# Rows of 64 KB in three buffers, loads on SyncE's queue and stores on ScalarE's in a written-out order

## The chip, the cores and the metric

The kernel runs on one core of a Trainium2 chip. The metric is device time in microseconds (us). A transfer "lands" when all its data has arrived and an engine that waits for it may start. In the profile lines DVE is VectorE, ACT ScalarE, POOL GpSimd, SP SyncE, PE TensorE and PEld its weight loads; L77 is line 77 of the kernel, and a q after an engine's name is its queue of DMA issues. "Span" is the length of the one profiled execution; in the profiled runs of the kernels tried here the reported time is 1.7 to 2.2 us longer than the span. Ratios are those over the fast runs of both kernels in the same rounds, so they are not quite the ratio of the medians that are quoted.

## The reference

```python
x: 16 x 3 x 512 x 512 float32; factor = 1.5
mean = np.mean(x, axis=(2, 3), keepdims=True)
return np.clip(mean + factor * (x - mean), 0, 1)
```

There are 48 images of 1 MiB (262,144 pixels). Each must be read whole before its first pixel can be written, because the mean is needed. The traffic is 50.33 MB in and 50.33 MB out, whatever the kernel does.

## The kernel before

Eleven tiles of four images and two of two images; a row (one partition) is 32 KB in the large tiles. VectorE sums the rows, one small matmul adds the rows of an image and gives all of them the mean times (1 - factor), ScalarE computes relu(factor * x + bias), VectorE clips at 1. Loads go out on SyncE's queue, stores on GpSimd's. A scheduler orders each engine's instructions.

```python
TILE_IMGS = [4] * 11 + [2, 2]
X_BUFS = 5
STORE_ENGINE = "gpsimd"
# ... [blockw: a 128 x 128 block-diagonal matrix of (1 - factor) / n_pix]
xpool = ctx.enter_context(tc.tile_pool(name="xpool", bufs=X_BUFS))
# ... [small pools]
for i, N in enumerate(TILE_IMGS):
    FREE = n_pix * N // P
    # ... [src, dst: FREE contiguous elements per partition]
    nc.sync.dma_start(out=xt, in_=src)
    nc.vector.tensor_reduce(out=rsum, in_=xt, axis=..., op=add)
    nc.tensor.matmul(pbias, blockw[N], rsum, start=True, stop=True)
    nc.scalar.copy(out=bias, in_=pbias)
    nc.scalar.activation(out=xt, in_=xt, func=Relu, bias=bias, scale=factor)
    nc.vector.tensor_scalar(out=xt, in0=xt, scalar1=1.0, scalar2=None, op0=min)
    store_eng.dma_start(out=dst, in_=xt)
```

## Time and profile before

| | before |
|---|---|
| time, median | 240.24 us (240.1 to 240.93, 3 runs) |
| span of the profiled run | 238.6 us |
| bytes moved, mean rate | 100.66 MB, 422 GB/s |
| busy: VectorE, ScalarE | 66%, 37% |
| a load and a store of 4.19 MB, steady state | 19.4 us |

The page of the kernel before: the busy times, then the span in 40 slices (DMA is the mean busy share of the 16 DMA engines in tenths, GB/s what they moved), then the packets.

```profile
span 238.6 us, 238 instructions
...
PE 7.4 (3%) x26; PEld 6.5 (3%) x26; DVE 156.5 (66%) x26; ACT 89.1 (37%) x27; POOL 10.3 (4%) x25
...
DMA  7999999999999999999999999999999999999995
GB/s 269 434 439 439 439 439 352 439 434 439 439 439 439 439 434 434 423 428 412 423 439 439 434 439 439 439 439 439 434 428 426 426 404 428 431 434 439 428 434 214
DMA packets 3744, 100.66 MB, mean 422 GB/s; under 512 B 416, under 2 KB 416, under 8 KB 416
```

The DMA row stands at 9 from the second slice to the last but one, and the rate is 434 to 439 GB/s where nothing disturbs it. No compute engine comes near that. The Trainium skill ("DMA: Bandwidth & Descriptors", Where 436 GB/s comes from) gives 435 GB/s as the ceiling of the ports through which DMA reaches SBUF, the on-chip memory; the trace shows 439, about 1% more. So the kernel before is bound by its bytes: 100.66 MB at 439 GB/s are 229.3 us, and start, end and dips take the other 9.

The groups of instructions of the kernel before: busy us and mean ns of one after the first bar, idle time of the engine before them after the second.

```profile
L77 DVE TENSOR_REDUCE rsum<-xt 128x1 f32<-128x8192 f32 x11 | 95.5, 8685 | 56.1 <-DMA xt<-in_x_dram 56.1
L90 ACT ACTIVATE xt<-xt,bias 128x8192 f32<-128x8192 f32 x11 | 78.4, 7124 | 0.4
L97 DVE TENSOR_SCALAR xt<-xt 128x8192 f32<-128x8192 f32 x11 | 48.6, 4417 | 0.0
...
L85 PE MATMUL pbias<-rsum,blockw 128*128 128x1 f32 x26 | 7.4, 355 | 209.5 <-DVE rsum L77 209.5
```

A 4 MB tile takes 8.7 us of reduce, 7.1 of relu and 4.4 of clip. These 20 us overlap with other tiles' transfers, so they cost nothing as long as DMA always has something queued. Stretches of the end of the kernel before: length, then busy us and number of instructions for PE, PEld, DVE, ACT, POOL, then clock, DMA share and GB/s.

```profile
195.00:206.00 11.00, 0.56 (x2) 0.50 (x2) 9.39 (x3) 7.35 (x3) 1.22 (x2) 1.00 0.99 420
206.00:216.00 10.00, 0.00 (x0) 0.00 (x0) 5.86 (x2) 0.00 (x0) 2.31 (x2) 1.00 0.97 419
216.00:226.00 10.00, 0.56 (x2) 0.50 (x2) 2.52 (x2) 3.87 (x2) 0.53 (x1) 1.00 1.03 442
226.00:236.00 10.00, 0.00 (x0) 0.00 (x0) 0.00 (x0) 0.00 (x0) 0.00 (x0) 1.00 0.94 403
```

The last load (2 MB) lands at 211.8 us and the last store is issued at 223.5, but DMA has older stores to move all the while: 419 to 442 GB/s.

### The profile page before, as it was taken

What the parts mean: (1) busy time and instruction counts of PE and PEld (TensorE: products, weight loads), DVE (VectorE), ACT (ScalarE), POOL (GpSimd) and SP (SyncE); (2) the same over time, 40 slices, a digit from 0 to 9 for tenths busy, and PEclk for the clock granted to TensorE, in tenths of its full rate; (3) what the DMA queues carried; (4) which work ended last, traced back from release to release, by engine and by line L of the source; (5) the groups of instructions that cost most, each with busy time, mean ns of one, the idle gap of its engine ahead of it and who ended that gap; (6) DMA issues with size and microseconds to landing.
All of it is one profiled execution on the core that took longest, in us unless ns stands there. A gap on an engine that the chain in (4) does not pass through costs nothing.

```text
span 238.6 us, 238 instructions
## 1 busy us (share of the span) xinstructions
PE 7.4 (3%) x26; PEld 6.5 (3%) x26; DVE 156.5 (66%) x26; ACT 89.1 (37%) x27; POOL 10.3 (4%) x25
## 2 busy tenths in 40 slices
PE   0000000000000000000000000000000000000000
PEld 0000000000000000000000000000000000000000
DVE  0088999999599079459629909917945979742300
ACT  2002966472906601900920650470190095406000
POOL 2000001000000000000000000000000000500000
DMA  7999999999999999999999999999999999999995
GB/s 269 434 439 439 439 439 352 439 434 439 439 439 439 439 434 434 423 428 412 423 439 439 434 439 439 439 439 439 434 428 426 426 404 428 431 434 439 428 434 214
DMA packets 3744, 100.66 MB, mean 422 GB/s; under 512 B 416, under 2 KB 416, under 8 KB 416
## 3 DMA queue, kind: packets, MB, share of 16 engines
q1 hardware_dynamic: 1872, 50.33, 49.4%
q0 software_dynamic: 1872, 50.33, 49.0%
HBM read 50.33 MB, written 50.33 MB: 422 GB/s over the span
## 4 chain that ended last, share of the span: by engine, by line
issue 38%; DMA 35%; DVE 18%; POOL 2%; POOLq 0%; SPq 0%
DMA xt<-in_x_dram 19%; DMA out_dram<-xt 16%; DVE rsum L77 11%; DVE xt L97 7%; POOL out_dram L104 2%; POOLq L137 0%; SPq L74 0%; POOLq L104 0%
## 5 line engine op out<-in xcount | busy, mean ns | idle before, releaser
L77 DVE TENSOR_REDUCE rsum<-xt 128x1 f32<-128x8192 f32 (+1 forms) x13 | 104.4, 8029 | 61.7 <-DMA xt<-in_x_dram 61.7
L90 ACT ACTIVATE xt<-xt,bias 128x8192 f32<-128x8192 f32 (+1 forms) x13 | 85.8, 6598 | 0.4
L97 DVE TENSOR_SCALAR xt<-xt 128x8192 f32<-128x8192 f32 (+1 forms) x13 | 53.2, 4091 | 5.0 <-ACT xt L90 5.0
L88 ACT COPY bias<-pbias 128x1 f32<-128x1 f32 x13 | 2.1, 160 | 130.6 <-PE pbias L85 130.6
L104 POOL DMA_DIRECT2D out_dram<-xt x13 | 9.0, 692 | 213.0 <-DVE xt L97 212.8
L85 PE MATMUL pbias<-rsum,blockw 128*128 128x1 f32 x26 | 7.4, 355 | 209.5 <-DVE rsum L77 209.5
L85 PEld LDWEIGHTS pbias<-rsum,blockw 128*128 128x128 f32 x26 | 6.5, 311 | 210.3 <-DVE rsum L77 107.1
L88 ACT ACT_TABLE_LOAD x1 | 1.3, 1283 | 0.8 <-PEq L123 0.8
L51 POOL MEMSET blockw<- 32x32 f32 (+1 forms) x6 | 0.8, 128 | 0.2
L49 POOL MEMSET blockw<- 128x128 f32 x2 | 0.3, 205 | 0.3 <-POOLq L123 0.3
L123 POOL MEMSET const-float32-0.0<- 128x1 f32 x1 | 0.1, 104 | 0.2 <-issue 0.2
L123 POOL MEMSET const-bfloat16-1.0<- 128x1 bf16 x1 | 0.1, 113 | 0.0
L123 POOL MEMSET const-uint8-127<- 128x1 uint8 x1 | 0.1, 113 | 0.0
L123 POOL MEMSET const-float32-1.0<- 128x1 f32 x1 | 0.1, 110 | 0.0
## 6 DMA issues: line engine op xcount, KB each, us to landing
xt<-in_x_dram SPq DMA_DIRECT2D x11, 4096.0 KB, 24.6
out_dram<-xt POOLq DMA_DIRECT2D x11, 4096.0 KB, 36.0
xt<-in_x_dram SPq DMA_DIRECT2D x2, 2048.0 KB, 19.5
out_dram<-xt POOLq DMA_DIRECT2D x2, 2048.0 KB, 19.1
```

Of the source, the lines that this page charges most:

```text
L49: nc.gpsimd.memset(wt, 0.0)
L51: nc.gpsimd.memset(wt[b * PPI : (b + 1) * PPI, b * PPI : (b + 1) * PPI], wconst)
L77: nc.vector.tensor_reduce(out=rsum, in_=xt, axis=mybir.AxisListType.X, op=mybir.AluOpType.add,)
L85: nc.tensor.matmul(pbias, blockw[N], rsum, start=True, stop=True)
L88: nc.scalar.copy(out=bias, in_=pbias)
L90: nc.scalar.activation(out=xt, in_=xt, func=mybir.ActivationFunctionType.Relu, bias=bias, scale=factor,)
L97: nc.vector.tensor_scalar(out=xt, in0=xt, scalar1=1.0, scalar2=None, op0=mybir.AluOpType.min,)
L104: store_eng.dma_start(out=dst, in_=xt)
L123: nc = _bacc.Bacc("TRN2", target_bir_lowering=False, num_devices=1)
```

## The change

It is meant to make the transfers as large as three buffers allow, to take the stores off GpSimd's software queue, and to fix the order of each engine's instructions by hand instead of leaving it to the scheduler. The sum is split: half of a row on VectorE, half on ScalarE. Relu and clip go in four chunks, so that they overlap within a tile.

```diff
-TILE_IMGS = [4] * 11 + [2, 2]
-X_BUFS = 5
-STORE_ENGINE = "gpsimd"
+ROW = 16384
+BUFS = 3
+HALF = ROW // 2
+CHUNK = 4096
+JUNK = 2048
 ... [block matrix written in another way; pools of 2]
+    def load(t):
+        xt = xpool.tile([P, ROW], f32, name="xt")
+        nc.sync.dma_start(out=xt, in_=dram(x_f, t))
+    def compute(t):
+        nc.vector.tensor_reduce(out=sums[:, 0:1], in_=xt[:, 0:HALF], ...)
+        for j in range(n_act):
+            nc.scalar.activation(out=junk, in_=xt[:, a : a + JUNK], func=Act.Copy,
+                                 accum_out=sums[:, 1 + j : 2 + j])
+        for j in range(1 + n_act):
+            nc.tensor.matmul(pbias, blockw, sums[:, j : j + 1], start=j == 0, stop=j == n_act)
+        nc.scalar.copy(out=bias, in_=pbias)
+        for c in range(0, ROW, CHUNK):
+            nc.scalar.activation(out=part, in_=part, func=Act.Relu, bias=bias, scale=factor)
+            nc.vector.tensor_scalar(out=part, in0=part, scalar1=1.0, scalar2=None, op0=Alu.min)
+    def store(t):
+        nc.scalar.dma_start(out=dram(out_f, t), in_=tiles.pop(t))
+    with tc.manual_schedule():
+        for t in range(min(BUFS, n_tiles)):
+            load(t)
+        for t in range(n_tiles):
+            compute(t)
+            store(t)
+            if t + BUFS < n_tiles:
+                load(t + BUFS)
```

With 16,384 elements per partition a tile is eight images, 8.39 MB, and there are six tiles.

More of the change, by code (lines that the diff above doesn't have):

```diff
@@ L5 @@
 import concourse.tile as tile
-from concourse import bass_utils, mybir
+from concourse import mybir
 from concourse._compat import with_exitstack
-TILE_IMGS = [4] * 11 + [2, 2]
-X_BUFS = 5
-STORE_ENGINE = "gpsimd"
+P = 128
+ROW = 16384
[3 more added lines that the diff above has]
+JUNK = 2048
 @with_exitstack
@@ L23 @@
     nc = tc.nc
-    P = 128
+    f32 = mybir.dt.float32
+    Alu = mybir.AluOpType
+    Act = mybir.ActivationFunctionType
     B, C, H, W = x.shape
-    n_img = B * C
-    n_pix = H * W
+    n_img, n_pix = B * C, H * W
+    ppi = n_pix // ROW
+    per_tile = P // ppi
+    n_tiles = n_img // per_tile
+    assert ppi * ROW == n_pix and per_tile * n_tiles == n_img
     factor = float(factor)
-    f32 = mybir.dt.float32
-    assert sum(TILE_IMGS) == n_img
-    NMAX = max(TILE_IMGS)
+    wconst = (1.0 - factor) / float(n_pix)
@@ L36, with dram @@
     x_f = x.rearrange("b c h w -> (b c h w)")
     out_f = out.rearrange("b c h w -> (b c h w)")
-    wconst = (1.0 - factor) / float(n_pix)
+    def dram(ap, t):
+        return bass.AP(tensor=ap.tensor, offset=t * P * ROW, ap=[[ROW, P], [1, ROW]])
     consts = ctx.enter_context(tc.tile_pool(name="consts", bufs=1))
-    blockw = {}
-    for N in sorted(set(TILE_IMGS)):
-        wt = consts.tile([P, P], f32, name=f"blockw{N}")
-        PPI = P // N
-        if N == 1:
-            nc.gpsimd.memset(wt, wconst)
-        else:
-            nc.gpsimd.memset(wt, 0.0)
-            for b in range(N):
-                nc.gpsimd.memset(wt[b * PPI : (b + 1) * PPI, b * PPI : (b + 1) * PPI], wconst)
-        blockw[N] = wt
@@ L54 @@
-    xpool = ctx.enter_context(tc.tile_pool(name="xpool", bufs=X_BUFS))
-    rpool = ctx.enter_context(tc.tile_pool(name="rpool", bufs=12))
-    bpool = ctx.enter_context(tc.tile_pool(name="bpool", bufs=12))
-    psum = ctx.enter_context(tc.tile_pool(name="psum", bufs=8, space=bass.MemoryType.PSUM))
-    if STORE_ENGINE == "sync":
-        store_eng = nc.sync
-    elif STORE_ENGINE == "act":
-        store_eng = nc.scalar
-    else:
-        store_eng = nc.gpsimd
-    pix_off = 0
-    for i, N in enumerate(TILE_IMGS):
-        FREE = n_pix * N // P
-        npix_tile = n_pix * N
-        xt = xpool.tile([P, NMAX * n_pix // P], f32, name="xt")[:, :FREE]
-        src = bass.AP(tensor=x_f.tensor, offset=pix_off, ap=[[FREE, P], [1, FREE]])
-        dst = bass.AP(tensor=out_f.tensor, offset=pix_off, ap=[[FREE, P], [1, FREE]])
-        nc.sync.dma_start(out=xt, in_=src)
-        rsum = rpool.tile([P, 1], f32)
+    xpool = ctx.enter_context(tc.tile_pool(name="xpool", bufs=BUFS))
@@ new lines @@
+    jpool = ctx.enter_context(tc.tile_pool(name="jpool", bufs=1))
+    rpool = ctx.enter_context(tc.tile_pool(name="rpool", bufs=2))
+    bpool = ctx.enter_context(tc.tile_pool(name="bpool", bufs=2))
+    psum = ctx.enter_context(tc.tile_pool(name="psum", bufs=2, space=bass.MemoryType.PSUM))
+    blockw = consts.tile([P, P], f32, name="blockw")
+    nc.gpsimd.memset(blockw, 0.0)
+    for a in range(0, P, 2 * ppi):
+        mid, end = a + ppi, a + 2 * ppi
+        nc.gpsimd.memset(blockw[a:end, mid:end], wconst)
+        nc.gpsimd.memset(blockw[a:mid, mid:end], 0.0)
+        nc.gpsimd.memset(blockw[a:mid, a:mid], wconst)
@@ L77 @@
+    tiles = {}
+    def load(t):
+        xt = xpool.tile([P, ROW], f32, name="xt")
+        nc.sync.dma_start(out=xt, in_=dram(x_f, t))
+        tiles[t] = xt
+    def compute(t):
+        xt = tiles[t]
+        n_act = (ROW - HALF) // JUNK
+        sums = rpool.tile([P, 1 + n_act], f32, name="sums")
         nc.vector.tensor_reduce(
-            out=rsum,
-            in_=xt,
-            axis=mybir.AxisListType.X,
-            op=mybir.AluOpType.add,
-        )
-        pbias = psum.tile([P, 1], f32)
@@ L85 @@
-        nc.tensor.matmul(pbias, blockw[N], rsum, start=True, stop=True)
-        bias = bpool.tile([P, 1], f32)
-        nc.scalar.copy(out=bias, in_=pbias)
-        nc.scalar.activation(
-            out=xt,
-            in_=xt,
-            func=mybir.ActivationFunctionType.Relu,
-            bias=bias,
-            scale=factor,
-        )
-        nc.vector.tensor_scalar(
-            out=xt,
-            in0=xt,
-            scalar1=1.0,
-            scalar2=None,
-            op0=mybir.AluOpType.min,
-        )
@@ L104 @@
-        store_eng.dma_start(out=dst, in_=xt)
-        pix_off += npix_tile
+            out=sums[:, 0:1], in_=xt[:, 0:HALF], axis=mybir.AxisListType.X, op=Alu.add
+        )
+        for j in range(n_act):
+            junk = jpool.tile([P, JUNK], f32, name="junk")
+            a = HALF + j * JUNK
+            nc.scalar.activation(
+                out=junk, in_=xt[:, a : a + JUNK], func=Act.Copy, accum_out=sums[:, 1 + j : 2 + j]
+            )
+        pbias = psum.tile([P, 1], f32, name="pbias")
@@ new lines, in compute @@
+        for j in range(1 + n_act):
+            nc.tensor.matmul(pbias, blockw, sums[:, j : j + 1], start=j == 0, stop=j == n_act)
+        bias = bpool.tile([P, 1], f32, name="bias")
+        nc.scalar.copy(out=bias, in_=pbias)
+        for c in range(0, ROW, CHUNK):
+            part = xt[:, c : c + CHUNK]
+            nc.scalar.activation(out=part, in_=part, func=Act.Relu, bias=bias, scale=factor)
+            nc.vector.tensor_scalar(out=part, in0=part, scalar1=1.0, scalar2=None, op0=Alu.min)
```

## The prediction

> **What bounds it now.** The DMA engines. The page moves 100.66 MB at 422 GB/s; its slices show DMA at 0.9 or more nearly throughout, at 434 to 439 GB/s, with VectorE busy 66% and ScalarE 37%. The Trainium skill ("DMA: Bandwidth & Descriptors", Where 436 GB/s comes from) gives 435 GB/s for a core's 16 engines; the trace agrees (439). At 439 GB/s the bytes need 229.3 of the 238.6 us span. By the windows about 2.5 us go at the start, 2.5 at the end, the rest in dips (352 GB/s where the first store begins). So nothing can win more than 2 to 3%. No compute wait matters: in steady state a 4 MB load and store complete every 19.4 us, VectorE working 13.1 of it.
>
> **What the change does.**
> - Six tiles of 8.39 MB (19.1 us of DMA each way at 439 GB/s) instead of eleven of 4.19 and two of 2.10 MB. Bytes are unchanged.
> - Three buffers: a load waits for the landed store three tiles earlier.
> - Stores move from GpSimd's software queue to ScalarE's hardware queue. The same page (Issuing engines are not separate DMA queues) says that all queues share the same 16 engines: no bandwidth gained. The trace agrees: loads and stores, both backlogged, advance equally, 19.4 us per tile.
> - Half of the sum goes to ScalarE (4 x 2048), relu and clip in four chunks. Engines work tile by tile in written order: no reduce of the next tile before this tile's last clip.
>
> **Compute of one tile, landing to store issue.** Reduce of 8192: 8.69 us, ScalarE's sums about as long (estimate 4 x 2.1, from 7.12 us at 8192 and 3.71 at 4096). Five matmuls instead of one, and the bias copy: 1 to 2.5 us (one pair takes 0.56). Relu 4 x 3.65; last clip 2.29. Sum about 28 us, under the 38.2 us in which DMA moves one tile in and one out: mid-run DMA stays full.
>
> **Critical path.** Load 0 lands at 22.7 us (the second load's landing before). Store 0 issues at about 51, store 1 at about 80, just as store 0 ends: hardly a gap. Then load t+3 shares with store t+1 and queues stay filled until load 5 lands. By then six loads, four stores and a bit of the fifth have moved, 85 MB: at before's pace (83.3 MB by 195 us) 198 to 200 us. Store 4 then runs alone and ends near 215 to 218, while tile 5 computes until about 227: a DMA hole of about 10 us. Then store 5 alone, 19 to 21 us (the last stores of before ran at 400 to 450 GB/s), plus about 3 us of issue and landing. Span about 250; the reported time lies 1.6 above the span, as now.
>
> **Predicted: 251.5 us, 8 in 10 between 246.5 and 256.5. Faster by over 2%: 0.03; within 2%: 0.09; slower by over 2%: 0.88.**
>
> **What would show it.** Slices: DMA full until about 215, a hole of 8 to 12 us, a last full stretch of about 20; last load landing at 196 to 201; the chain of waits ending in last load, about 28 us of tile 5's compute, last store; relu chunks 3.6 to 3.7 us; ScalarE sums 2.0 to 2.3 us each; mid-run still about 435 to 440 GB/s.
>
> **What would make it wrong.** Loads taking more than half of the bandwidth: load 5 lands earlier, the hole shrinks, 240 to 245 us. A hardware store queue that lifts the dips: 3 to 4 us less. A DMA gap after store 0 because tile 1 computes longer, or ScalarE held up at its store's issue: a few us more.

## The result

| | before | after |
|---|---|---|
| time, median | 240.17 us (4 runs) | 254.78 us (253.09 to 258.41, 4 runs); the three fast ones 253.09 to 255.92, mean 254.22 |
| ratio | | 1.0581 (95%: 1.0524 to 1.0638) |
| span of the profiled run | 238.6 us | 251.3 us |
| mean rate | 422 GB/s | 401 GB/s |
| packets | 3744 | 1729 |
| busy: VectorE, ScalarE | 66%, 37% | 43%, 55% |

The change makes the kernel 5.8% slower. The same lines of the page, after:

```profile
span 251.3 us, 317 instructions
...
PE 13.7 (5%) x60; PEld 13.2 (5%) x60; DVE 107.0 (43%) x30; ACT 137.3 (55%) x79; POOL 1.4 (1%) x17
...
DMA  8979899799989899989999899997999979303994
GB/s 334 501 334 501 355 480 501 334 355 480 480 355 501 344 396 428 501 355 480 407 428 501 355 480 407 429 501 344 490 417 417 501 344 490 167 0 167 501 490 177
DMA packets 1729, 100.67 MB, mean 401 GB/s; under 512 B 192, under 2 KB 192, under 8 KB 192
```

Two things are to be seen. First, the rates swing between 334 and 501. That is partly the ruler: there are half as many packets, so each now carries a row of 64 KB and, at a sixteenth of 439 GB/s, keeps its engine for 2.4 us (an estimate), a good part of a 6.3 us slice. Bytes are counted in such lumps: 16 packets of 64 KB in a slice of 6.28 us are 167 GB/s, and 334 and 501 are two and three times that. Only longer stretches can be compared. Secondly, near the end there are slices with 167, 0 and 167 GB/s. The stretches of the end, after:

```profile
206.00:211.00 5.00, 0.90 (x5) 0.90 (x5) 4.05 (x1) 3.37 (x4) 0.00 (x0) 1.00 0.97 419
211.00:216.00 5.00, 1.40 (x7) 1.31 (x7) 0.00 (x0) 3.54 (x2) 0.00 (x0) 1.00 0.97 419
216.00:229.50 13.50, 0.00 (x0) 0.00 (x0) 9.18 (x4) 11.13 (x4) 0.00 (x0) 1.00 0.00 0
229.50:240.00 10.50, 0.00 (x0) 0.00 (x0) 0.00 (x0) 0.00 (x0) 0.00 (x0) 1.00 0.93 399
```

From 216 to 229.5 us not a byte moves, while ScalarE (11.1 us of 13.5) and VectorE (9.2) work on the last tile. These 13.5 us can be laid beside the whole difference of the two spans, 12.7 us. The chain of waits says what goes on in them (start, length, what):

```profile
157.73 43.54 DMA xt<-in_x_dram
...
201.36 8.70 DVE sums L77
...
210.10 2.31 PE pbias L88 x10
...
212.43 0.17 ACT bias L90
...
212.62 14.52 ACT xt L93 x4
...
227.16 2.29 DVE xt L94
```

The last load is issued at 157.7 us, since only then its buffer has been stored, and lands at 201.3. Then reduce, matmuls, bias copy, four relus and the last clip follow one another, 28.2 us, and only at 229.5 the store of the whole tile is issued; it lands 20.7 us later. The store of the tile before was all that DMA had in the meantime, and it was done at 216. The groups, after:

```profile
L93 ACT ACTIVATE xt<-xt,bias 128x4096 f32<-128x4096 f32 x24 | 87.0, 3697 | 0.2
L83 ACT ACTIVATE junk<-xt 128x2048 f32<-128x2048 f32 x24 | 45.8, 1910 | 71.8 <-DMA xt<-in_x_dram 65.8
L94 DVE TENSOR_SCALAR xt<-xt 128x4096 f32<-128x4096 f32 x24 | 55.1, 2294 | 61.5 <-ACT xt L93 61.5
L77 DVE TENSOR_REDUCE sums<-xt 128x1 f32<-128x8192 f32 x6 | 52.1, 8683 | 61.0 <-DMA xt<-in_x_dram 61.0
L88 PE MATMUL pbias<-sums,blockw 128*128 128x1 f32 x60 | 13.7, 354 | 198.7 <-DVE sums L77 198.7
...
L83 ACT ACTIVATION_READ_ACCUMULATOR junk<-xt 128x1 f32 x24 | 4.5, 186 | 0.0
```

Each part costs about what the trace before led to expect. The Trainium skill ("ScalarE: Activation LUTs", What ACT_TABLE_LOAD costs) gives 186 ns + 0.833 ns per element for an ACTIVATE with immediate scale and bias and about 280 ns + 0.833 ns per element with a bias per partition. An estimate worked out from that is 1892 ns for 2048 and 3692 ns for 4096 elements. The trace has 1910 and 3697.

### The profile page after: what moved, and what is told of

It is laid out like the page before. It is cut to its first block, busy times and chain, and to the rows that moved or that the text cites. A ratio compares the mean times of both kernels' runs of the same rounds, so it can differ in the third digit from the quotient of the medians.

```text
span 251.3 us, 317 instructions
## 1 busy us (share of the span) xinstructions
PE 13.7 (5%) x60; PEld 13.2 (5%) x60; DVE 107.0 (43%) x30; ACT 137.3 (55%) x79; POOL 1.4 (1%) x17
## 2 busy tenths in 40 slices
DMA packets 1729, 100.67 MB, mean 401 GB/s; under 512 B 192, under 2 KB 192, under 8 KB 192
## 4 chain that ended last, share of the span: by engine, by line
DMA 42%; ACT 18%; another core or an unknown queue 15%; DVE 13%; PE 3%; issue 0%; SPq 0%; DVEq 0%
DMA xt<-in_x_dram 26%; ACT xt L93 17%; DMA out_dram<-xt 16%; DVE sums L77 10%; PE pbias L88 3%; DVE xt L94 3%; ACT bias L90 0%; SPq L70 0%; DVEq L77 0%
## 5 line engine op out<-in xcount | busy, mean ns | idle before, releaser
L93 ACT ACTIVATE xt<-xt,bias 128x4096 f32<-128x4096 f32 x24 | 87.0, 3697 | 0.2
L83 ACT ACTIVATE junk<-xt 128x2048 f32<-128x2048 f32 x24 | 45.8, 1910 | 71.8 <-DMA xt<-in_x_dram 65.8
L94 DVE TENSOR_SCALAR xt<-xt 128x4096 f32<-128x4096 f32 x24 | 55.1, 2294 | 61.5 <-ACT xt L93 61.5
L77 DVE TENSOR_REDUCE sums<-xt 128x1 f32<-128x8192 f32 x6 | 52.1, 8683 | 61.0 <-DMA xt<-in_x_dram 61.0
L88 PE MATMUL pbias<-sums,blockw 128*128 128x1 f32 x60 | 13.7, 354 | 198.7 <-DVE sums L77 198.7
L88 PEld LDWEIGHTS pbias<-sums,blockw 128*128 128x128 f32 x60 | 13.2, 329 | 199.1 <-DVE sums L77 167.7
L90 ACT COPY bias<-pbias 128x1 f32<-128x1 f32 x6 | 1.0, 159 | 17.0 <-PE pbias L88 17.0
L83 ACT ACTIVATION_READ_ACCUMULATOR junk<-xt 128x1 f32 x24 | 4.5, 186 | 0.0
L63 POOL MEMSET blockw<- 16x16 f32 x4 | 0.4, 104 | 0.2
L64 POOL MEMSET blockw<- 16x16 f32 x4 | 0.4, 104 | 0.0
## 6 DMA issues: line engine op xcount, KB each, us to landing
xt<-in_x_dram SPq DMA_DIRECT2D x6, 43.5
```

The costliest lines, as they stand in the source:

```text
L63: nc.gpsimd.memset(blockw[a:mid, mid:end], 0.0)
L64: nc.gpsimd.memset(blockw[a:mid, a:mid], wconst)
L77: nc.vector.tensor_reduce(out=sums[:, 0:1], in_=xt[:, 0:HALF], axis=mybir.AxisListType.X, op=Alu.add)
L83: nc.scalar.activation(out=junk, in_=xt[:, a : a + JUNK], func=Act.Copy, accum_out=sums[:, 1 + j : 2 + j])
L88: nc.tensor.matmul(pbias, blockw, sums[:, j : j + 1], start=j == 0, stop=j == n_act)
L93: nc.scalar.activation(out=part, in_=part, func=Act.Relu, bias=bias, scale=factor)
```

## The experiments

The theory: DMA sets the time, and what the change adds is a stretch in which DMA has nothing to do, because the last tile is so large that its compute outlasts the stores that were still queued. Put as a sum, the hole is the time from the last landing to the last store's issue, less the time that DMA needs for the stores still waiting at that landing. The rivals: the 64 KB rows make DMA slower throughout; ScalarE's queue is worse than GpSimd's; the written-out order costs; the number of buffers alone is to blame.

### The last tile stored in four chunks

```diff
     def store(t):
-        nc.scalar.dma_start(out=dram(out_f, t), in_=tiles.pop(t))
+        xt = tiles.pop(t)
+        if t < n_tiles - 1:
+            nc.scalar.dma_start(out=dram(out_f, t), in_=xt)
+            return
+        for c in range(0, ROW, CHUNK):
+            dst = ...  # columns c to c + CHUNK of tile t
+            nc.sync.dma_start(out=dst, in_=xt[:, c : c + CHUNK])
```

> The changed kernel, but the last tile is stored in four column chunks from SyncE's queue, each as soon as its clip is done. Theory (the whole loss is the DMA hole from 216 to 229.5 us, in which tile 5 computes and nothing can be stored): the first chunk can go at about 219 us instead of 229.5, the hole shrinks to about 3 us, span about 240.5, time about 242 (0.95 of the changed kernel). Rival (the 64 KB rows or ScalarE's store queue make DMA slower throughout): the tail gives back less than 3 us, time 250 or more.

Measured: 243.37 us (243.1 to 243.74), ratio to before 1.0132 (1.0094 to 1.0169), span 242.0. The stretches:

```profile
216.00:219.00 3.00, 0.00 (x0) 0.00 (x0) 1.28 (x1) 3.00 (x2) 0.00 (x0) 1.00 0.25 109
219.00:222.00 3.00, 0.00 (x0) 0.00 (x0) 1.70 (x2) 3.00 (x2) 0.00 (x0) 1.00 0.41 175
222.00:230.00 8.00, 0.00 (x0) 0.00 (x0) 5.39 (x3) 6.49 (x2) 0.00 (x0) 1.00 1.01 426
```

The first chunk goes out at 220.0 us, and from 222 on DMA is full. From 216 to 222 us, 109 and 175 GB/s over 3 us each make 0.85 MB, what full DMA moves in 2 us: the hole is worth about 4 us instead of 13.5. The means of the fast runs fall by 10.8 us, from 254.22 to 243.39, and the hole by about 9.5; the 1.3% that is left goes with the hole that is left. So nearly the whole loss sat in the hole. Both chunking and the queue of this one store changed. The run with GpSimd's stores below shows no effect of the queue there; SyncE's was not tried by itself.

### Half the tile, twice the buffers

```diff
-ROW = 16384
-BUFS = 3
+ROW = 8192
+BUFS = 6
```

> The changed kernel with rows of 32 KB and six buffers: same buffer bytes, same queues, same written order, half the tile. Theory (granularity): compute of one tile falls from 28 to about 16 us and at the last load's landing several computed tiles are still to be stored, so no DMA hole: span 237 to 239, time 238.5 to 241, level with before. Rival (hardware store queue or written order costs): 248 or more, DMA slices below 435 GB/s in mid-run.

Measured: 240.19 us, ratio to before 0.9997 (0.9954 to 1.0041), 421 GB/s. The last load lands at 207.9 us and the last store is issued at 223.8, and from the middle of the run to the last slice but one the slices stay at 411 to 439 GB/s. Stores on ScalarE's queue, the split sum, the chunks (now two of a row) and the written order are all still there and cost nothing. What costs is the size of the tile, or how few of them fit.

### Half the tile, still three buffers; and four

```diff
-ROW = 16384
+ROW = 8192
```

> The changed kernel with rows of 32 KB, still three buffers. Theory: with three buffers, when the last load lands only one tile (9.6 us alone) is left to store while the last tile computes about 16 us: a hole of about 6 us, half of that of the changed kernel, plus a gap of 2 to 3 us after the first store: time 246 to 249. If it were the tile size alone and not how many tiles lie ready: 239 to 241. If it were the buffer count alone and not the size: 254.

Measured: 255.06 us (253.95 to 255.55), ratio 1.0609: as slow as the changed kernel. This misses the 246 to 249 that I had expected. The stretches show in which way:

```profile
41.00:47.00 6.00, 0.00 (x0) 0.00 (x0) 4.70 (x3) 3.25 (x3) 0.00 (x0) 1.00 0.59 202
124.50:183.60 59.10, 4.32 (x18) 4.07 (x18) 27.02 (x9) 34.39 (x21) 0.00 (x0) 1.00 0.98 413
...
234.00:241.00 7.00, 0.00 (x0) 0.00 (x0) 4.59 (x2) 4.58 (x2) 0.00 (x0) 1.00 0.00 0
```

The hole at the end is there and has the expected size: the last load lands at 225.0 us, the store before it is done at 234, the last one is issued at 240.9, so 7 us stand empty. But the middle loses as much again. At 41 to 47 us only 202 GB/s move, and from 124.5 to 183.6 the mean is 413 GB/s against 433 in the copies below. The chain of waits runs through store, load and compute of every third tile without a break; one round of it (start, length, what):

```profile
60.44 21.05 DMA out_dram<-xt
...
81.56 23.03 DMA xt<-in_x_dram
...
104.71 4.43 DVE sums L77
...
110.85 7.32 ACT xt L93 x2
...
118.19 2.31 DVE xt L94
...
120.52 22.05 DMA out_dram<-xt
```

Every third store is issued at 60.4, 120.5, 181.5 and 240.9 us, so one buffer's round takes about 59 to 61 us, while DMA needs 57.3 for three tiles both ways at 439 GB/s (an estimate from the rate of before). The reading is that the round, and not DMA, then sets the pace; it asks that one more buffer fill the middle, which the next run shows. (The changed kernel's round, from the store at 78.8 us to the one at 190.8, takes 112 us beside 114.7: it just fits, and 426 GB/s move in it, the rate of the 64 KB copy below from 60 to 220 us.) The middle of the run had been checked only by comparing the compute of one tile with its DMA. Here that comparison comes out well too (15.7 us under 19.1), so it is not enough: the round has to fit as well.

Four buffers were tried with

```diff
-ROW = 16384
-BUFS = 3
+ROW = 8192
+BUFS = 4
```

> Rows of 32 KB with four buffers, between the runs with three (255.1) and six (240.2). Theory: at the last landing two tiles (2 x 9.6 us of DMA) are still to be stored, more than the 15.8 us from landing to store issue, so no tail hole, and four buffers also cover load, compute and store in mid-run: 239.5 to 242.5. If the loss shrank evenly with the buffers: about 250.

Measured: 244.5 us (243.29 to 244.61), ratio 1.0173 (1.0142 to 1.0204), span 242.5. This misses the 239.5 to 242.5 that I had expected; whether it is slower by 2% is unclear. The middle is full now (433 to 434 GB/s from 100 to 215 us). The hole is smaller, not gone:

```profile
225.00:228.00 3.00, 0.00 (x0) 0.00 (x0) 1.91 (x1) 3.00 (x1) 0.00 (x0) 1.00 0.56 240
228.00:230.00 2.00, 0.00 (x0) 0.00 (x0) 1.78 (x1) 0.18 (x1) 0.00 (x0) 1.00 0.00 0
```

The last load lands at 214.7 us and the last store is issued at 230.5, after 15.8 us. In 225 to 228 us 240 GB/s flow, what full DMA moves in 1.7 us, so it ran dry at about 226.7 us. The stores that waited at the landing were worth 12 us, not the two full tiles (19 us) that I had counted: part of them had already moved beside the last load. My count of the waiting tiles was too high. The sum 15.8 - 12 = 3.8 is bookkeeping, since the 12 are read off at the point where DMA ran dry. The test is the time: against the run with six buffers the ratio rises by 0.0176, 4.2 us, beside a hole of 3.8.

| kernel | last landing | last store issued | DMA dry from | hole |
|---|---|---|---|---|
| changed: 64 KB rows, 3 buffers | 201.3 | 229.5 | 216 | 13.5 |
| 32 KB rows, 3 buffers | 225.0 | 240.9 | 234 | 7 |
| 32 KB rows, 4 buffers | 214.7 | 230.5 | 226.7 | 3.8 |
| 32 KB rows, 6 buffers | 207.9 | 223.8 | never | none |

### The queue of the stores

The changed kernel with GpSimd's queue:

```diff
-        nc.scalar.dma_start(out=dram(out_f, t), in_=tiles.pop(t))
+        nc.gpsimd.dma_start(out=dram(out_f, t), in_=tiles.pop(t))
```

> The changed kernel with its stores on GpSimd's software queue as before had them, nothing else. Theory (tail hole from tile size and buffers): 252 to 256 us, hole of about 13 us unchanged. Rival (hardware store queue costs): 240 to 246.

Measured: 254.7 us, ratio to before 1.0595 (1.0565 to 1.0625), beside 1.0581 for the changed kernel; mean rate 398 GB/s. One slice again moves nothing, with 72 and 166 GB/s beside it; from 218 to 231 us no byte moves, the hole of about 13 us that was expected. The queue makes no difference here.

The kernel before with ScalarE's queue:

```diff
-STORE_ENGINE = "gpsimd"
+STORE_ENGINE = "act"
```

> The kernel before with its stores on ScalarE's queue, nothing else. Theory (queue is innocent): 238 to 242 us, within 1% of before; ScalarE held at its store's issue costs nothing because DMA is backlogged. Rival (hardware store queue costs): 246 or more.

Measured: 271.88 us (271.46 to 273.35), ratio 1.1329. That is 30 us over what I expected, and by its number it is the rival's (246 or more). The timeline of ScalarE (start, length, engine, line, what; ACTq is ScalarE's queue of DMA issues) shows why:

```profile
113.16 21.14 ACT L90 ACTIVATE xt<-xt,bias 128x8192 f32<-128x8192 f32 x3
133.71 17.60 ACTq L104 DMA_DIRECT2D out_dram<-xt  x3
151.35 0.22 ACT L88 COPY bias<-pbias 128x1 f32<-128x1 f32 x2 [17.05 <-DVE xt L97]
...
179.31 21.15 ACT L90 ACTIVATE xt<-xt,bias 128x8192 f32<-128x8192 f32 x3
198.54 13.34 ACTq L104 DMA_DIRECT2D out_dram<-xt  x3
```

The scheduler had bunched ScalarE's work: two or three relus, then two or three stores. At 133.7 us it comes to three stores at once, the last of which waits until 151.3 us for its clip; the next relus wait for their reduce until 179.3, and no store can be issued before 198.5. The slices of this run fall to 160, 34, 0 and 78 GB/s, each time before a bunch. Whether that is the queue or the order, the next run tells. It has the same kernel with each engine's order written out: reduce of tile t+1 ahead of the clip of tile t, relu of t+1 ahead of the store of t.

```diff
-STORE_ENGINE = "gpsimd"
+STORE_ENGINE = "act"
 ...
+    with tc.manual_schedule():
+        for i, N in enumerate(TILE_IMGS):
+            cur = first(i, N, pix_off)    # load, reduce, matmul, copy, relu
+            if prev is not None:
+                second(*prev)             # clip, store
+            prev = cur
+            pix_off += n_pix * N
+        second(*prev)
```

> The kernel before with its stores on ScalarE's queue, as in the run that took 271.9 us, but with a written-out order: reduce of tile t+1 ahead of the clip of tile t, relu of t+1 ahead of the store of t. Theory: not the queue but the order in which the scheduler put ScalarE's stores (in bunches of two and three, behind relus that wait for loads) cost 32 us: 238.5 to 242 us here. Rival (ScalarE's store queue costs): 255 or more.

Measured: 239.64 us (239.4 to 239.91), ratio to before 0.9982 (0.9961 to 1.0004), 424 GB/s. So the order cost the 32 us, not the queue. The two belong together: stores on an engine that also computes stand in that engine's line.

### The changed kernel in the scheduler's order

```diff
-    with tc.manual_schedule():
+    if True:
```

> The changed kernel, its order left to the scheduler, nothing else. Theory: ScalarE's stores then stand behind sums of the next tile, which wait for loads (from the third tile on the relu of tile t itself stands behind a sum of tile t+1), so stores start late and DMA runs dry in mid-run too: 260 to 270 us. Rival (written order is what costs the changed kernel its time): under 250.

Measured: 253.0 us (252.74 to 253.32), ratio to before 1.0539 (1.0516 to 1.0562), mean rate 401 GB/s. I had expected 260 or more, so this is a miss. In this order relus do stand behind sums of the next tile, as expected: store 2 is issued at 133.5 us, against 106.8 in the changed kernel. But held-back stores let the loads run ahead, and the last load lands at 189.0 us instead of 201.3. The tail hole shrinks to about 2 us, and DMA is thin in several places earlier: against the 426 GB/s of the 64 KB copy below, the stretches from 80 to 133.5 us and from 157 to 189 (393 GB/s) lose about 8 us (an estimate). Three of the stretches:

```profile
80.00:114.00 34.00, 1.17 (x4) 1.00 (x4) 7.46 (x4) 12.16 (x8) 0.00 (x0) 1.00 0.97 395
...
126.00:133.50 7.50, 0.39 (x2) 0.39 (x2) 6.37 (x3) 7.47 (x5) 0.00 (x0) 1.00 0.83 358
...
227.00:229.00 2.00, 0.00 (x0) 0.00 (x0) 2.00 (x1) 0.00 (x0) 0.00 (x0) 1.00 0.00 0
```

The mean rate is the same 401 GB/s, so the loss is the same size, differently spread. The written-out order is worth nothing to speak of in this kernel (the two were not run in the same rounds, so a difference of half a per cent stays open), while in the kernel before with ScalarE's stores an order is worth 32 us.

### The sizes alone, in the kernel before

```diff
-TILE_IMGS = [4] * 11 + [2, 2]
-X_BUFS = 5
+TILE_IMGS = [8] * 6
+X_BUFS = 3
 ... [block matrix for eight images, written as in the changed kernel]
```

> The kernel before with six tiles of eight images in three buffers (the sizes of the changed kernel), GpSimd's queue, whole-tile compute, no written order. Theory: sizes alone bring the loss, and the split compute of the change even softens it: reduce 17.4, relu 13.9, clip 8.8 us, 41 us from landing to store issue, so a gap near 61 to 68 us and a tail hole of 25 us or more; time 262 to 272. Rival (sizes innocent): 238 to 244.

Measured: 265.67 us (265.65 to 265.82), ratio 1.1062 (1.1038 to 1.1085). The sizes of the changed kernel, with nothing else of it, cost 25 us. DMA runs dry in more than one place: the slices show 0 near 63 us, where I had expected the first gap, 179 and 159 near 191 and 159 near 221, so not one tail hole of 25 us but several smaller ones. The time lies in the expected 262 to 272, but not by the path that I had expected. The rest of the change then brings the loss down to 14 us. The split sum and the chunks, which shorten a tile's compute from 41 us (an estimate, in the expectation above) to 28.2, are the likely reason; they were not tried one by one.

### Copies without compute

```diff
-            compute(t)
```

These give a wrong result: each tile is stored as it was loaded. They measure what the transfers take by themselves. Rows of 64 KB in three buffers:

> Wrong result on purpose: the changed kernel without its compute, so that a tile is stored when it has landed. Measures what DMA alone takes with 64 KB rows, three buffers and these two queues. Theory (DMA rate unharmed): span 232 to 237, time 234 to 239. Rival (64 KB rows slow DMA): 245 or more.

Rows of 32 KB in six buffers:

> Wrong result on purpose: as the 64 KB copy, with rows of 32 KB in six buffers. Theory: within 1% of the 64 KB copy. Rival (row size matters): over 2% faster than it.

Rows of 32 KB in three buffers:

> Wrong result on purpose: copy without compute, rows of 32 KB, three buffers. Tells which of the two makes the 64 KB copy (241.7) 2 us slower than the 32 KB copy in six buffers (239.7). Row size: 239 to 240.3. Number of buffers: 241.3 or more. Without compute a load and a store of 9.6 us each need only two buffers, so I expect 239.5.

| copy | time | ratio to before |
|---|---|---|
| 64 KB rows, 3 buffers | 241.71 us | 1.0064 (1.0039 to 1.0089) |
| 32 KB rows, 6 buffers | 239.69 us | 0.9976 (0.9953 to 0.9999) |
| 32 KB rows, 3 buffers | 239.37 us | 0.9967 (0.9941 to 0.9992) |

The 64 KB copy is 2.7 us above the range that I had expected, the 32 KB copies are where the expectations had them. The rival's 245 us for the 64 KB rows is not reached either. Three things follow. The kernel before, at 240.2 us, is within half a per cent of a copy that computes nothing: there was next to nothing left to win. No version that computes beats it clearly; the quickest, its own stores on ScalarE's queue in a written order, has 1 inside its interval. Three buffers are enough for a copy, so buffers by themselves cost nothing; they are short only when compute stands between load and store. And the 64 KB rows (with the 8.39 MB tiles that go with them) cost 2 us, a per cent, as DMA alone. Whether it is the row or the size of the transfer was not separated, and why it costs is open.

The two terms add up to within 1 or 2 us: 241.7 for the copy and 13.5 for the hole make 255.2 us, and the fast runs took 254.22 on average; with the last tile in chunks 241.7 and 4 make 245.7, and 243.4 was measured. Before the hole nothing is lost against that copy: up to 201.3 us, the last landing, the changed kernel and the 64 KB copy both moved 427 GB/s.

## Why the prediction was right

The prediction named 251.5 us and the measured 254.78 lies within its range. The mechanism is the one foretold, a DMA hole while the last tile computes, but three of its signs came out beside what it gave for them: the hole (8 to 12 us), the rate in mid-run and, by a hair, the last landing (196 to 201). Point by point:

- *DMA bounds the kernel, and no more than 2 to 3% can be won.* Right, and the copies sharpen it: less than half a per cent.
- *Mid-run DMA stays full, at 435 to 440 GB/s.* Full it was, but at 428 GB/s from 22.6 to 216 us. And the ground given for it, 28 us of compute under 38.2 us of DMA, was not enough, as the three buffers of 32 KB rows show: that the round of 64 KB rows fits (112 us beside 114.7) was not checked, and was in part luck.
- *Compute of one tile, about 28 us.* 28.2: 8.7 for the reduce, 2.3 for the ten passes of the five matmuls, 0.2 for the copy, 14.5 for the relus, 2.3 for the last clip.
- *Store 0 at about 51, store 1 at about 80.* 50.8 and 78.8.
- *Last load at 198 to 200.* 201.3. The term "at before's pace" was right: 427 GB/s up to that landing, as in the kernel before up to 195 us. It was the bytes that were undercounted: 427 GB/s over 201.3 us are 86 MB, not 85. The fifth store was further on than I had reckoned, though 1 MB is also one lump of the count.
- *A hole of about 10 us.* 13.5, from 216 to 229.5. The two ends were foretold as "215 to 218" and "about 227"; the first was at its early end, the second late by the 2 us of the last load. Put as the sum of the theory: compute of 28.2 us was foretold well, but the store still under way at the last landing was worth 14.7 us, not the 17 or so of the prediction (198 to 200 until 215 to 218). That is the count of waiting stores again, too high as in the run with four buffers.
- *Last store alone, 19 to 21 us and about 3 for issue and landing.* 21.8 from its issue to the end of the span, 20.7 of it to the landing: a little less than I counted, which offsets part of the misses above.
- *Span about 250, the time 1.6 above it.* The span is 251.3 and its run took 253.09, 1.8 more. But that was the fastest of the runs, and the mean of the three fast ones is 254.22. So of the 2.7 us by which 251.5 fell short of that mean, 1.3 are the span, 0.3 the step from the span to the time, and 1.1 the spread from run to run. The changed kernel's fast runs spread wider (253.09 to 255.92) than those of any other kernel here (2 us at most); why is open.
- *ScalarE's queue brings and costs nothing.* Right for bandwidth. The Trainium skill ("DMA: Bandwidth & Descriptors", Issuing engines are not separate DMA queues) says that all issuing engines share the same 16 DMA engines; the ratios agree with that: 1.0595 beside 1.0581 for the changed kernel, and 0.9982 for the kernel before. What I did not see is that the choice of engine also chooses whose order the store stands in: 271.9 us.
- *Loads taking more than half of the bandwidth*, which I had named as what could make it wrong, did not come about: the last load took 43.5 us beside stores, against 21.8 for the first. Of the 43.5 it stood 4.9 behind the load before it; its 8.39 MB in the other 38.7 us are 217 GB/s, half of the 434 that moved then.

## What to carry to other kernels

In a kernel bound by DMA, ask of the last tile: how long from its landing to its store, and how much is still queued for DMA at that moment? If the first is longer, the difference is lost, however full DMA is before. For the second, count the bytes still to move and not the tiles: both forecasts here counted too much. Large transfers make it worse on both sides, since they lengthen the tile's compute and leave fewer tiles to queue; store the last tile in pieces, or keep tiles small and many. And check that one buffer's whole round of load, compute and store fits into the time that DMA needs for all buffers.

If stores are issued from an engine that computes, look at where they stand in its order. A copy without compute shows in one run how much there is to win at all.

## What the Trainium skill lacked or had wrong

- "DMA: Bandwidth & Descriptors" (Rules for kernel authors) asks for at least 1 MiB per DMA and names no other side to it. Here 8.39 MB transfers with 64 KB rows copy in 241.71 us, 4.19 MB ones with 32 KB rows in 239.37 us (both with three buffers): larger was 1% slower.
- The same page (Where 436 GB/s comes from) says that for transfers between HBM and SBUF the HBM side, about 358 GB/s, binds. With one core running, the kernels here moved 373 to 424 GB/s over their whole span, the slowest included, and the kernel before 439 from 60 to 99 us. The figure of about 425 for a core streaming alone in "HBM Reference" is nearer, and the 439 lie above it too.
- The same page (Issuing engines are not separate DMA queues) says that issuing from several engines only saves the time to initiate. What it nowhere spells out is the price when the issuing engine also computes, since a store then waits in that engine's order: 271.9 us in the scheduler's order, 239.64 in a written one.
- No page has the condition for the end of a run, compute of the last tile against the stores still queued: 13.5, 7, 3.8 and 0 us of idle DMA in four kernels that differ only in row length and buffers.
